# A hybrid decoder block on one core: w_down's difference blocks made in the first stage, and the low parts of k loaded once into half-zero tiles

## The chip, the cores and the metric

The kernel runs on one core of a Trainium2 chip. The core has four engines that the kernel programs separately: TensorE (PE in the profile, with PEld for its weight loads), VectorE (DVE), ScalarE (ACT) and GpSimd (POOL). A fifth, SyncE (SP), issues every DMA of this kernel from one queue, in order. Each engine runs its own instructions strictly in order and waits where one of them needs something that isn't there yet. The metric is the device time of one launch in microseconds; the median of 3 runs before the change is 2561.39 us (2550.47 to 2562.06).

## The reference, cut to what matters

The input x is 2048 tokens by 1024 channels, in float32. One layer:

```python
h = rmsnorm(x, g_mix)
p = h @ w_in                          # 1024 x 2560
a_val, a_gate, b_u, b_v, c_q, c_k, c_v = split(p)
y_a = conformer_conv(a_val, a_gate, ...)      # GLU, causal depthwise conv of 31, layernorm, silu
y_b = chunked_sgu(b_u, b_v, ...)              # gelu, layernorm, 128 x 128 causal mixing
y_c = stick_breaking_attention(c_q, c_k, c_v) # 8 heads of 64; z = q k^T / 8, causal
x = x + concat(rms(y_a), rms(y_b), rms(y_c)) * g_out @ w_out
h = rmsnorm(x, g_ffn)
up = causal_dwconv(h @ w_up)                  # 1024 x 5632, conv width 3
gate, val = split(up)
x = x + (silu(gate) * val) @ w_down           # 2816 x 1024
return rmsnorm(x, g_final)
```

## The kernel before, in words

All products are float32 made of float32r parts. A matrix a is split into a high part (a cast on ACT) and a low part (a minus its high part, on POOL or DVE), and a product is three matmuls: high times high, high times low, low times high (`mm3`, L115 to L117). The work has three stages.

**First stage, 0 to about 530 us.** The input projection, in two halves of 1024 tokens. For each half the columns of w_in come in five groups of 512 (`load_w`): the GLU (columns 0), branch B (512), k (1536), q (1024), v (2048). A group is four tiles `raw` of 512 KB; each is split by ACT (L120, `wh`) and POOL (L121, `wl`). There are two `raw` buffers and five pairs `wh`, `wl`, so only the first tile of a group can be ready while the group before it is in use; the other three follow as PE gives up the old ones. Tokens of x are loaded into the tiles `xi` (pool `xp`, four buffers of 512 KB), normed and transposed (`ptn`). Beside the matmuls DVE runs the convolution of branch A (L344, 31 taps, spread by the generator `conv`), and POOL norms branch B (L292, L295). q, k and v are stored in high and low parts to DRAM: qh_d, ql_d, kh_d, kl_d, v_d.

**Attention, about 515 to 1190 us.** 320 steps: four query blocks of 512 (qs), four head pairs (pr), the key blocks back from the diagonal (kc), two heads (hd), four rows of queries (j). `front` makes z with two matmuls of 128 rows: the stationary tile q of a head holds the high part on 64 rows and the low part on the other 64; it meets `kA` or `kB` (the high part of k, twice, on both halves) in L754 and `lA` or `lB` (the low part, twice) in L757. Then a sigmoid (`om`, ACT L759) and a cumulative product (DVE L762 and L767). Six steps later the result is transposed (`pat`, L780) and split into `ah` and `al`: for two of four on DVE (L793), for two on POOL (L790). Two steps after that it meets v (`po`, L802 and L803). A set of key tiles is loaded by `load_kv`: eight DMAs of 128 KB (four of kh_d, four of kl_d) and one of 512 KB (`vv`), two sets deep. Between the steps the output projection of earlier rows fills PE (`out_proj`, tiles `pab`), with its own loads of y, x and w_out. From step 40 on, every 20th step calls `wd_gen`: `down_blocks` (L605) loads two row blocks of w_down (512 KB each), makes four differences with POOL (L613 to L616) and stores them to wd_d (four DMAs of 256 KB). There are 11 such blocks; the last stage needs them.

**Feed-forward, about 1200 us to the end.** Up and down projections, each with seven block products in place of eight; `down_weights` (L1145) reads wd_d.

What sets the order. The source says in which order work is recorded; a scheduler then lays each engine's instructions out by a timeline of its own, so an engine's queue isn't quite in the order of the source. A tile's next use waits for all readers of its last one.

Of the kernel before, what the change touches and what calls it, by code (L numbers as in the profile page):

```python
# [8 lines left out]
F32 = mybir.dt.float32  # L9
# [6 lines left out]
P = 128  # L16
# [4 lines left out]
def kernel(  # L21
# [68 lines left out]
    def dma32(dst, src):  # L90
        nc.sync.dma_start(dst.bitcast(F32), src.bitcast(F32))
# [259 lines left out]
    def advance(gen, n):  # L351
        for _ in range(n):
            next(gen, None)
# [30 lines left out]
    def branch_b_tail(uv, vh, vl, hf, q4):  # L384
# [14 lines left out]
        branch_rms(yb)  # L399
        return lambda: store_t(yb, 2, hf * HALF + q4 * 512)  # L400

    xs = load_x(0, 0)
    constants()
    V.memset(glu[:, :, 0:HALO], 0.0)
# [42 lines left out]
    def load_kv(tiles, kc, pr):  # L447
        kA, kB, lA, lB, vv = tiles
        k_s = slice(kc * 512, (kc + 1) * 512)
        for hd, th_, tl_ in ((0, kA, lA), (1, kB, lB)):  # L450
            hr = slice(64 * hd, 64 * hd + 64)
            for r in (slice(0, 64), slice(64, 128)):
                dma32(th_[r], kh_d[pr, hr, k_s])
                dma32(tl_[r], kl_d[pr, hr, k_s])
        dma32(
            vv,
            v_d[kc * 4 : kc * 4 + 4, :, pr * 256 : (pr + 1) * 256].rearrange(
                "n p c -> p n c"
            ),
        )  # L460
        return tiles

    for hf in range(2):
# [21 lines left out]
        for q4 in range(2):  # L485
            uv = bp.tile([P, 4, 512], F32, tag="uv", name="uv", bufs=2)
            for j in range(4):
                ps = proj_d(w, hT[q4], j)
                A.activation(uv[:, j, :], ps, AF.Gelu)
                advance(conv, 2)  # L490
                tick()
            uvs.append((uv, *branch_b_norm(uv)))


        for c0, hd, ld in ((1536, kh_d, kl_d), (1024, qh_d, ql_d)):
            w = load_w(c0)
            if hf == 1 and c0 == 1024:

                pre = [
                    bp.tile([P, 4, 512], F32R, tag="uv", name=f"pre{i}", bufs=2)  # L500
                    for i in range(2)
                ]
                first_q = load_q((pre[0][:, 0, :], pre[0][:, 1, :]), 0, 0)
                first_kv = load_kv(
                    (
                        pre[0][:, 2, :], pre[0][:, 3, :], pre[1][:, 0, :],
                        pre[1][:, 1, :],
                        pre[1][:, 2:4, :].rearrange("p a (n c) -> p (a n) c", c=256),
                    ),
                    0, 0,  # L510
                )
            for ct in range(NPAIR):
                for ch in range(2):
                    ps = proj_t(w, ct, hT[ch])
                    eh = ep.tile([P, 512], F32R, tag="eh", name="eh")
                    el = ep.tile([P, 512], F32R, tag="el", name="el")
                    A.copy(eh, ps)
                    V.tensor_tensor(el, ps, eh, op=ALU.subtract)
                    t0 = hf * HALF + ch * 512
                    dma32(hd[ct, :, t0 : t0 + 512], eh)  # L520
                    dma32(ld[ct, :, t0 : t0 + 512], el)
                    advance(conv, 2 if c0 == 1536 else 3)
                    tick()
                    if c0 == 1536 and ct in (0, 2) and ch == 1:
                        after(4, branch_b_tail(*uvs[ct // 2], hf, ct // 2))
# [68 lines left out]
    def load_wo(f):  # L594
# [5 lines left out]
        split_pool(wh, wl, raw)  # L600
        wo_h.append(wh)
        wo_l.append(wl)

    def down_blocks():

        for f in range(NFH):
            r0 = xo.tile([P, D], F32, tag="wd0", name="wd0", bufs=1)
            r1 = xo.tile([P, D], F32, tag="wd1", name="wd1", bufs=1)
            nc.sync.dma_start(r0, w_down_r[f])
            nc.sync.dma_start(r1, w_down_r[NFH + f])  # L610
            b11, b12, b21, b22 = r0[:, 0:512], r0[:, 512:D], r1[:, 0:512], r1[:, 512:D]
            t3 = xo.tile([P, 512], F32, tag="t3", name="wd3", bufs=1)
            G.tensor_tensor(t3, b22, b12, op=ALU.subtract)  # L613
            G.tensor_tensor(b12, b12, b11, op=ALU.subtract)
            G.tensor_tensor(b22, b22, b12, op=ALU.subtract)
            G.tensor_tensor(b21, b21, b22, op=ALU.subtract)  # L616
            for i, t_ in enumerate((b12, b22, t3, b21)):
                nc.sync.dma_start(wd_d[i, :, f, :], t_)
            yield

    def store_blocks(n, he, ho, eng):

# [29 lines left out]
    def out_proj(qs, g, kept=()):  # L652
# [6 lines left out]
        for j in range(4):  # L659
            n = qs * 4 + j  # L660
            x1, (yh, yl) = nxt, ys.pop(0)
            for nh in range(2):
# [57 lines left out]
                        store_blocks(n, even, h, V if qs == NQ - 1 else G)  # L720
                yield

    class Pair:


# [11 lines left out]
    def front(p, kc, hd, j):  # L737
# [2 lines left out]


        if kc not in p.kv:
            kt = [
                kv.tile([P, 512], F32R, tag=n, name=n) for n in ("kA", "kB", "lA", "lB")
            ]
            kt.append(kv.tile([P, 4, 256], F32R, tag="vv", name="vv"))
            p.kv[kc] = load_kv(kt, kc, p.pr)
        kt, lt = p.kv[kc][hd], p.kv[kc][2 + hd]
# [149 lines left out]
    rms_at = {}  # L898
    ready = [out_proj(0, 0), out_proj(1, 0)]
    last_y = []  # L900
    wd_gen = down_blocks()
    for s_ in range(4 * NU + LAG_V):
        if s_ < 4 * NU:
            u, j = divmod(s_, 4)
# [11 lines left out]
                load_vend()  # L916
            if WO_0 <= s_ < WO_0 + 8 * WO_S and (s_ - WO_0) % WO_S == 0:
                load_wo((s_ - WO_0) // WO_S)
        if s_ >= 40 and s_ % 20 == 0:
            next(wd_gen, None)  # L920
        if s_ in rms_at:
            qs = rms_at[s_]
            rcs[qs] = rms_c(sqs[qs])
# [414 lines left out]
```

## Time and profile before

| | us |
|---|---|
| median of 3 runs | 2561.39 |
| profiled execution | 2565.55 |
| its span, first to last instruction | 2563.8 |
| first stage, 0 to 530: PE busy | 493.28 |
| 520 to 640: PE busy | 87.74 of 120 |
| 640 to 960: PE busy | 292.80 of 320 |
| 960 to 1160: PE busy | 190.61 of 200 |
| 1200 to the end: PE busy | 1323.72 of 1364 |

The page reads from the top: the busy time of each engine, then the span in 40 slices of 64 us, in which a digit is a share in tenths. A busy time doesn't say what bounds a stretch; for that the tables by stretch and the lists of waits are read. "PEclk" is the granted TensorE clock as a share of full speed (1.00 is 2.4 GHz, 0.50 is 1.2 GHz). The DMA share is the mean busy share of the 16 DMA engines, so a share near 1 says that no more can be moved in that stretch.

### The profile page before, as it was taken

What the parts mean: (1) busy time and instruction counts of PE and PEld (TensorE: products, weight loads), DVE (VectorE), ACT (ScalarE), POOL (GpSimd) and SP (SyncE); (2) the same over time, 40 slices, a digit from 0 to 9 for tenths busy, and PEclk for the clock granted to TensorE, in tenths of its full rate; (3) what the DMA queues carried; (4) which work ended last, traced back from release to release, by engine and by line L of the source; (5) the groups of instructions that cost most, each with busy time, mean ns of one, the idle gap of its engine ahead of it and who ended that gap; (6) DMA issues with size and microseconds to landing.
All of it is one profiled execution on the core that took longest, in us unless ns stands there. A gap on an engine that the chain in (4) does not pass through costs nothing.

```text
span 2563.8 us, 33236 instructions
## 1 busy us (share of the span) xinstructions
PE 2417.0 (94%) x11139; PEld 1965.9 (77%) x11139; DVE 1857.1 (72%) x2360; ACT 1202.9 (47%) x2138; POOL 1220.7 (48%) x941
## 2 busy tenths in 40 slices
PE   7999999968999889998799999999989999999998
PEld 5878778746777777776588888888867888888887
DVE  3881595356889888995688988874558888888555
ACT  4333522255667657774444444454344344345542
POOL 2433552445457453656154444565424444447551
PEclk9999999979999989998999999999999999999999
DMA  4245426389999998876333333397652333337962
GB/s 138 84 147 168 160 83 181 132 238 261 297 292 288 263 263 220 239 224 207 115 95 106 108 95 106 116 334 230 180 181 78 98 107 104 98 107 224 301 185 100
DMA packets 418235, 445.69 MB, mean 174 GB/s; under 512 B 23922, under 2 KB 301694, under 8 KB 418063
## 3 DMA queue, kind: packets, MB, share of 16 engines
q1 hardware_dynamic: 418063, 443.55, 58.0%
q8 instruction: 89, 1.46, 0.3%
q14 instruction: 83, 0.68, 0.1%
HBM read 305.57 MB, written 137.89 MB: 173 GB/s over the span
## 4 chain that ended last, share of the span: by engine, by line
PE 76%; DMA 8%; DVE 5%; issue 3%; POOL 3%; ACT 2%; SPq 1%; POOLq 0%; DVEq 0%; ACTq 0%
PE prod L115 11%; PE prod L117 11%; PE prod L116 11%; PE pd L117 5%; PE pd L115 5%; PE pd L116 5%; PE pat L780 3%; PE pjt L115 3%; PE pjt L117 3%; PE pjt L116 3%; PE pz L754 2%; PE po L803 1%; PE pab L115 1%; PE pz L757 1%; PE po L802 1%
## 5 line engine op out<-in xcount | busy, mean ns | idle before, releaser
L121 POOL TENSOR_TENSOR wl<-raw,wh 128x512 fp32r<-128x512 f32 (+1 forms) x260 | 383.4, 1477 | 560.6 <-ACT wh L120 548.5
L115 PE MATMUL prod<-thh,wh 128*128 128x512 f32 x1232 | 483.8, 393 | 13.1 <-DVE thl L1049 13.1
L117 PE MATMUL prod<-thh,wl 128*128 128x512 f32 x1232 | 485.1, 394 | 0.0
L116 PE MATMUL prod<-thl,wh 128*128 128x512 f32 x1232 | 482.6, 392 | 0.0
L120 ACT CAST wh<-raw 128x512 fp32r<-128x512 f32 (+1 forms) x260 | 177.4, 684 | 311.8 <-PE prod L116 178.4
L121 POOL TENSOR_TENSOR dwl<-raw,dwh 128x512 fp32r<-128x512 f32 x154 | 223.0, 1479 | 134.5 <-ACT dwh L120 106.2
L115 PEld LDWEIGHTS prod<-thh,wh 128*128 128x128 f32 x1232 | 232.4, 189 | 64.3 <-DVE thl L1049 15.2
L790 POOL TENSOR_TENSOR al<-ar,ah 128x512 fp32r<-128x512 f32 (+2 forms) x160 | 178.7, 1119 | 207.9 <-ACT ah L788 172.3
L116 PEld LDWEIGHTS prod<-thl,wh 128*128 128x128 f32 x1232 | 232.2, 188 | 52.2
L117 PEld LDWEIGHTS prod<-thh,wl 128*128 128x128 f32 x1232 | 232.3, 189 | 50.1
L767 DVE TENSOR_TENSOR_SCAN om<-om,pz 128x512 f32<-128x512 f32 x192 | 240.0, 1269 | 30.3 <-ACT om L759 29.1
L115 PE MATMUL pd<-dwh,sah 128*128 128x512 f32 x616 | 241.2, 392 | 1.3 <-DVE thl L1049 1.2
L117 PE MATMUL pd<-dwh,sal 128*128 128x512 f32 x616 | 242.0, 393 | 0.0
L116 PE MATMUL pd<-dwl,sah 128*128 128x512 f32 x616 | 240.4, 390 | 0.0
L1179 DVE TENSOR_TENSOR sal<-ar,sah 128x512 fp32r<-128x512 f32 x168 | 151.3, 913 | 122.6 <-ACT sah L1178 108.9
L1119 DVE SCALAR_TENSOR_TENSOR cv<-u,vec,cv 128x1024 f32<-128x1024 f32 x176 | 222.5, 1286 | 13.8 <-ACT cv L1117 12.1
L759 ACT ACTIVATE om<-pz 128x512 f32<-128x512 f32 (+2 forms) x320 | 168.6, 544 | 72.6 <-PE pz L757 69.1
L1066 DVE TENSOR_TENSOR u<-prod,u 128x512 f32<-128x512 f32 x220 | 147.2, 686 | 65.5 <-PE prod L117 62.8
L780 PE MATMUL pat<-ident,om 128*128 128x128 f32 x1088 | 179.6, 282 | 5.5 <-DVE al L793 3.7
L780 PEld LDWEIGHTS pat<-ident,om 128*128 128x128 f32 x1088 | 138.7, 145 | 40.9 <-DVE al L793 9.9
L121 POOL TENSOR_TENSOR wl<-s,wh 128x512 fp32r<-128x512 f32 x88 | 122.0, 1387 | 97.5 <-ACT wh L120 97.5
L1178 ACT CAST sah<-ar 128x512 fp32r<-128x512 f32 x168 | 97.1, 583 | 147.8 <-PE pd L116 106.3
(282 smaller groups left out, 5229.6 us busy)
## 6 DMA issues: line engine op xcount, KB each, us to landing
raw<-in_w_up_dram SPq DMA_DIRECT2D x88, 512.0 KB
ar<-s_d SPq DMA_DIRECT2D x112, 256.0 KB
s_d<-act SPq DMA_DIRECT2D x110, 256.0 KB
raw<-in_w_in_dram SPq DMA_DIRECT2D x40, 512.0 KB
raw<-wd_d SPq DMA_DIRECT2D x40, 512.0 KB
vv<-v_d SPq DMA_DIRECT2D x39, 512.0 KB
x_d<-x SPq DMA_DIRECT2D x32, 512.0 KB
raw<-in_w_down_dram SPq DMA_DIRECT2D x30, 512.0 KB
```

The costliest lines, as they stand in the source:

```text
L115: T.matmul(ps, lh, rh, start=start, stop=False)
L116: T.matmul(ps, lh, rl, start=False, stop=False)
L117: T.matmul(ps, ll, rh, start=False, stop=stop)
L120: A.copy(hi, src)
L121: G.tensor_tensor(lo, src, hi, op=ALU.subtract)
L759: A.activation(om, pz[:, :w_], AF.Sigmoid, scale=-0.125)
L767: V.tensor_tensor_scan(om[:, ::-1], om[:, ::-1], pz[:, ::-1], initial=p.carry[hd, j], op0=ALU.mult, op1=ALU.bypass,)
L780: T.transpose(pt[:, j * P : (j + 1) * P], a4[j][:, b * P : (b + 1) * P], ident)
L790: G.tensor_tensor(al[:, c_], ar[:, c_], ah[:, c_], op=ALU.subtract)
L1066: V.tensor_tensor(dst, ps, other, op=ALU.add)
L1119: V.scalar_tensor_tensor(cv, u[:, j : j + HALF], cw(j), cv, op0=ALU.mult, op1=ALU.add)
L1179: V.tensor_tensor(lo, ar, hi, op=ALU.subtract)
```

## The change

`down_blocks` moves to the first stage. It takes its two tiles from the pool of `xi`, needs no third tile (the differences are made in place, in another sequence), and yields twice a block: after the loads, and after the stores. It is called 12 times in each half: once after every second row of branch B's projection and once after every second product of k and of q. That makes 24 calls for the 22 halves of 11 blocks. The calls in the attention go.

`load_kv` stores the low part of k once, on the 64 rows where the stationary tile holds the high part of q; the other 64 rows of `lA` and `lB` are zeroed once and stay zero. For that `lA` and `lB` become two fixed pairs, used in turn, where they were tiles of a pool with two buffers. With it the product of the two low parts, which was part of z before, is left out.

```diff
+    def down_blocks():
+        for f in range(NFH):
+            r0 = xp.tile([P, D], F32, tag="xi", name="wd0")
+            r1 = xp.tile([P, D], F32, tag="xi", name="wd1")
+            nc.sync.dma_start(r0, w_down_r[f])
+            nc.sync.dma_start(r1, w_down_r[NFH + f])
+            yield
+            b11, b12, b21, b22 = r0[:, 0:512], r0[:, 512:D], r1[:, 0:512], r1[:, 512:D]
+            for i, t_, u_, v_ in (
+                (0, b12, b12, b11), (1, b22, b22, b12), (3, b21, b21, b22),
+                (2, b11, b22, b11),
+            ):
+                G.tensor_tensor(t_, u_, v_, op=ALU.subtract)
+                nc.sync.dma_start(wd_d[i, :, f, :], t_)
+            yield
+    wd_gen = down_blocks()
...
             for r in (slice(0, 64), slice(64, 128)):
                 dma32(th_[r], kh_d[pr, hr, k_s])
-                dma32(tl_[r], kl_d[pr, hr, k_s])
+            dma32(tl_[hr], kl_d[pr, hr, k_s])
...
                 A.activation(uv[:, j, :], ps, AF.Gelu)
                 advance(conv, 2)
+                advance(wd_gen, j % 2)
...
+                G.memset(pre[1][64:128, 0, :].bitcast(F32), 0.0)
+                G.memset(pre[1][0:64, 1, :].bitcast(F32), 0.0)
                 first_q = load_q((pre[0][:, 0, :], pre[0][:, 1, :]), 0, 0)
...
                     advance(conv, 2 if c0 == 1536 else 3)
+                    advance(wd_gen, ch)
...
+    lows, turn_l = [], [0]
+    for i in range(2):
+        lows.append([kv.tile([P, 512], F32R, tag=f"{n}{i}", name=f"{n}{i}", bufs=1) for n in ("lA", "lB")])
+        for hd, t_ in enumerate(lows[i]):
+            zr = slice(64 * (1 - hd), 64 * (1 - hd) + 64)
+            G.memset(t_[zr].bitcast(F32), 0.0)
...
-            kt = [
-                kv.tile([P, 512], F32R, tag=n, name=n) for n in ("kA", "kB", "lA", "lB")
-            ]
+            kt = [kv.tile([P, 512], F32R, tag=n, name=n) for n in ("kA", "kB")]
+            kt += lows[turn_l[0] % 2]
+            turn_l[0] += 1
...
-        if s_ >= 40 and s_ % 20 == 0:
-            next(wd_gen, None)
```

How the queues stand. SP's queue in the first stage, before, from the constants of the feed-forward on: `xi` are the tokens of the second half, `raw` the rest of the weights up to k's first products, whose stores come next.

```order
19 L180 DMA r__596<-in_ffn_conv_b_dram 44x128
20 L211 DMA xi<-in_x_dram 128x1024 x4
21 L246 DMA raw<-in_w_in_dram 128x2x512 x8
22 L91 DMA kh_d<-eh 128x512 x2
23 L91 DMA kl_d<-el 128x512 x2
```

The same place now; a wd tile with a number is one block's half.

```order
19 L180 DMA r__596<-in_ffn_conv_b_dram 44x128
20 L407 DMA wd_685<-in_w_down_dram 128x1024
21 L408 DMA wd_686<-in_w_down_dram 128x1024
22 L407 DMA wd_837<-in_w_down_dram 128x1024
23 L408 DMA wd_838<-in_w_down_dram 128x1024
24 L417 DMA wd_d<-wd_685 128x512
25 L417 DMA wd_d<-wd_686 128x512 x2
26 L417 DMA wd_d<-wd_685 128x512
27 L407 DMA wd_1022<-in_w_down_dram 128x1024
28 L417 DMA wd_d<-wd_837 128x512
29 L408 DMA wd_1023<-in_w_down_dram 128x1024
30 L246 DMA raw<-in_w_in_dram 128x2x512
```

The first six blocks now stand where the four tiles of tokens stood, with the weights between them; the tokens follow behind the sixth block.

POOL's queue at the change from the GLU's weights to branch B's, before: the `wl` are the low parts of weight tiles, `rs` and `uv` belong to branch B's norm.

```order
12 L194 AFFINE_SELECT wsm<-wsr 128x128 x4
13 L121 TENSOR_TENSOR wl<-raw,wh 128x1024 x4
14 L112 TENSOR_TENSOR rs_755<-tm_754,mhalf 128x4
15 L292 TENSOR_TENSOR uv<-uv,ln_119 128x4x256
16 L295 TENSOR_TENSOR uv<-uv,ln_120 128x4x256
```

The same place now.

```order
12 L194 AFFINE_SELECT wsm<-wsr 128x128 x4
13 L416 TENSOR_TENSOR wd_685<-wd_685 128x512
14 L416 TENSOR_TENSOR wd_686<-wd_686,wd_685 128x512
15 L416 TENSOR_TENSOR wd_686<-wd_686 128x512
16 L416 TENSOR_TENSOR wd_685<-wd_686,wd_685 128x512
17 L416 TENSOR_TENSOR wd_837<-wd_837 128x512
18 L121 TENSOR_TENSOR wl<-raw,wh 128x1024
19 L416 TENSOR_TENSOR wd_838<-wd_838,wd_837 128x512
20 L121 TENSOR_TENSOR wl<-raw,wh 128x1024
21 L416 TENSOR_TENSOR wd_1022<-wd_1022 128x512
22 L416 TENSOR_TENSOR wd_838<-wd_838 128x512
23 L416 TENSOR_TENSOR wd_837<-wd_838,wd_837 128x512
```

The splits of the weights, which stood together, now have differences between them, and all six blocks of this half are made by the second row of `uv`.

SP's queue in the attention, before, some way into the second query block.

```order
285 L91 DMA kA<-kh_d 64x512
286 L91 DMA lA<-kl_d 64x512
287 L91 DMA kA<-kh_d 64x512
288 L618 DMA wd_d<-wd_5069 128x512
289 L91 DMA lA<-kl_d 64x512
290 L91 DMA yh_d<-ych 128x512
291 L618 DMA wd_d<-wd_5065 128x512
```

And a like place now.

```order
371 L91 DMA kA<-kh_d 64x512 x2
372 L91 DMA lA_4199<-kl_d 64x512
373 L91 DMA yh_d<-ych 128x512
374 L91 DMA qA<-qh_d 64x512
```

One load of the low part stands where two stood, and the stores of wd_d are gone.

## Rows read from the trace of the kernel before

**Rows 1.** The page: the DMA share in tenths, 40 slices of 64 us.

```profile
DMA  4245426389999998876333333397652333337962
```

**Rows 2.** Stretches: busy us (count) of PE, PEld, DVE, ACT, POOL; clock; DMA share; GB/s.

```profile
520.00:640.00 120.00, 87.74 (x397) 68.40 (x396) 74.34 (x96) 63.01 (x142) 58.21 (x49) 0.84 0.97 253
640.00:960.00 320.00, 292.80 (x1524) 237.85 (x1523) 271.33 (x305) 206.50 (x432) 175.38 (x154) 0.95 0.97 280
960.00:1160.00 200.00, 190.61 (x1039) 154.15 (x1038) 181.42 (x197) 148.75 (x298) 109.33 (x92) 1.00 0.81 227
```

**Rows 3.** w_down's differences: ns, min/median/max, first and last start.

```profile
L613 POOL TENSOR_TENSOR wd<-wd,wd x11: 1262/1288/1300, 619.2 to 948.6; 128x512 f32<-128x512 f32 x11
```

**Rows 4.** Waits of PE, 520 to 640: us in total, times, longest.

```profile
PE pz L754 <- DMA kA<-kh_d: 12.6, 4, 4.8
```

**Rows 5.** Waits of PE, 640 to 960.

```profile
PE po L803 <- POOL al L790: 12.6, 5, 4.9
...
PE po L802 <- DMA vv<-v_d: 2.4, 1, 2.4
```

**Rows 6.** DMA, 520 to 640: bytes, then issues with count and size.

```profile
DMA packets 21229, 30.41 MB, mean 253 GB/s; under 512 B 2063, under 2 KB 11791, under 8 KB 21222
...
lA<-kl_d SPq DMA_DIRECT2D x14, 128.0 KB
...
lB<-kl_d SPq DMA_DIRECT2D x12, 128.0 KB
...
wd<-in_w_down_dram SPq DMA_DIRECT2D x2, 512.0 KB
wd_d<-wd SPq DMA_DIRECT2D x3, 256.0 KB
```

**Rows 7.** DMA, 640 to 960.

```profile
DMA packets 59211, 89.62 MB, mean 280 GB/s; under 512 B 5808, under 2 KB 31322, under 8 KB 59184
...
wd_d<-wd SPq DMA_DIRECT2D x41, 256.0 KB
...
wd<-in_w_down_dram SPq DMA_DIRECT2D x20, 512.0 KB
...
lB<-kl_d SPq DMA_DIRECT2D x40, 128.0 KB
...
lA<-kl_d SPq DMA_DIRECT2D x40, 128.0 KB
```

**Rows 8.** Two stretches of the first stage, columns as in Rows 2.

```profile
80.00:120.00 40.00, 40.00 (x178) 33.14 (x177) 36.47 (x45) 12.41 (x15) 16.61 (x8) 1.00 0.13 40
...
200.00:240.00 40.00, 40.00 (x180) 33.02 (x179) 3.73 (x8) 9.47 (x14) 12.17 (x7) 1.00 0.46 138
```

**Rows 9.** SP: the load of the second half's tokens before.

```profile
64.48 1.77 SPq L211 DMA_DIRECT2D xi<-in_x_dram  x4
```

**Rows 10.** The chain that ended last, 100 to 136 us: start, duration.

```profile
105.53 2.40 POOL uv L292
...
118.86 4.13 DMA raw<-in_w_in_dram
...
126.50 1.04 POOL rs L112
```

**Rows 11.** The same chain later: a store of 256 KB.

```profile
477.22 2.01 DMA vr_d<-vs
```

**Rows 12.** PE at the first change of weights: the first matmul with branch B's weights.

```profile
75.65 0.39 PE L115 MATMUL pjd<-wh,hTh 128*128 128x512 f32 x1
```

**Rows 13.** POOL at that change: start, duration.

```profile
73.61 4.76 POOL L121 TENSOR_TENSOR wl<-raw,wh 128x1024 fp32r<-128x1024 f32 x2 [26.90 <-ACT wh L120]
81.08 2.40 POOL L121 TENSOR_TENSOR wl<-raw,wh 128x1024 fp32r<-128x1024 f32 x1 [2.70 <-ACT wh L120]
```

**Rows 14.** POOL at the same change in the second half.

```profile
320.23 4.77 POOL L121 TENSOR_TENSOR wl<-raw,wh 128x1024 fp32r<-128x1024 f32 x2 [20.21 <-ACT wh L120]
```

**Rows 15.** Branch A's convolution on DVE: ns, min/median/max.

```profile
L344 DVE SCALAR_TENSOR_TENSOR pc<-glu,vec,pc x116: 1257/1290/1292, 72.6 to 413.3; 128x1024 f32<-128x1024 f32 x116
```

More of the change, by code (lines that the diff above doesn't have):

```diff
@@ L602, in load_wo @@
         wo_l.append(wl)
[L604 to L619, printed above, removed]
     def store_blocks(n, he, ho, eng):
@@ L900 @@
     last_y = []
-    wd_gen = down_blocks()
     for s_ in range(4 * NU + LAG_V):
```

## Prediction

> **What bounds the kernel now.** I read the page's slices first, then a table by stretch, the waits of PE in two of the stretches, and what the DMA engines moved in them. The slices show one plateau of full DMA engines, from the end of the first stage through two thirds of the attention [rows 1]. The stretches give it sizes [rows 2]: from 520 to 640 us the DMA share is 0.97, PE is busy for 87.74 of 120 us and its granted clock averages 0.84 of 2.4 GHz; from 640 to 960 the share is again 0.97, PE is busy for 292.80 of 320 at 0.95. From 960 to 1160, when the last of w_down's differences has started (at about 950 us [rows 3]), the share is 0.81 and PE busy for 190.61 of 200 at 1.00. So the attention has a part that is short of transfers and a part where PE is the bound, and the change takes bytes from the first. In 520 to 640 PE's waits say so: 12.6 us on kA [rows 4]. In 640 to 960 they say it only in part: 2.4 us on vv, but 12.6 on `al` from POOL [rows 5], in whose queue w_down's differences stand.
>
> **The base.** The sum is made against the profiled execution, 2565.55 us with a span of 2563.8. It stands 4.2 us above the median of the runs, 2561.39; I take that off at the end.
>
> **520 to 640 us.** What goes: half of the 26 loads of low parts, 13 x 0.131 = 1.70 MB; two loads of w_down, 1.05 MB; three stores to wd_d, 0.79 MB; together 3.54 of 30.41 MB [rows 6], at 253 GB/s 14.0 us. PE could take all of it, since it idles 120 - 87.74 = 32 us and loses 87.74 x 0.16 = 14 to the clock. I take two thirds, -9, since less than half of the idle time names a transfer [rows 4]. Bounds: 0 (PE waits for kA's loads, and those stay) and -18 (fewer waits bring the clock back as well).
>
> **640 to 960 us.** What goes: half of 80 low parts, 5.2 MB; 20 loads of w_down, 10.5 MB; 41 stores, 10.7 MB; together 26.5 of 89.62 MB [rows 7], at 280 GB/s 94 us. The other 63.1 MB need 225 us at that rate, so transfers no longer bound the stretch, and PE is late next. It issued 1524 matmuls here and 1039 in the 200 us that follow [rows 2]; at that rate 1524 take 293 us, 27 fewer. The other way: 292.80 x 0.95 = 278 us of full clock, at the later busy share of 190.61 / 200 = 0.953, give 292. The new stretch would move 63.1 MB in 292 us, 216 GB/s, under the 227 of the one it is compared with, and DVE would be busy for 271.33 / 292 = 0.93 against 181.42 / 200 = 0.91: the comparison is fair, with DVE a little short. POOL gives up 41 differences of 1.288 us [rows 3], 53 us, that stood before `al`; this works in the same 27 and is not added. I take three quarters, -20, as the two stretches don't run the same mix of fill and attention. Bounds: -5 (vv's wait and a fifth of `al`'s) and -30 (the clock as well).
>
> **After 960 us.** Only low parts go, where PE is already at 0.953 and its clock at 1.00 [rows 2]: -1, between 0 and -4. The feed-forward keeps its order and reads the same wd_d: 0.
>
> **The first stage pays.** 11 blocks come in, with two loads, four differences and four stores each, through SP's one queue and POOL's. The DMA engines have room, a share of 0.13 and 0.46 in two stretches [rows 8]. The question is who stands behind the blocks in the two queues.
>
> First half. The tokens' tiles come free at 64.5 us, when the next tokens were loaded [rows 9]; now two blocks are. With 4.13 us for a load of 512 KB [rows 10], 1.29 for a difference [rows 3], 2.01 for a store of 256 KB [rows 11] and about 1 for issues, a pair of tiles takes 4.1 + 5.2 + 2.0 + 1 = 12.3 us a turn, and two pairs work at once: 6.2 us a block, six in 37 us. From about 69 that is 106; four splits of weights share POOL meanwhile, 2.4 us each, so 106 to 115.
>
> Behind them stand the splits of branch B's weights. PE turned to those at 75.65 [rows 12]. It runs three products side by side (three PSUM tiles), 18 matmuls a tile, at 40.00 / 180 = 0.222 us each [rows 8]; the fourth tile's low part is needed after 54 of them, at 87.6, and was there at 81.08 + 2.40 = 83.5 [rows 13]. Now ten differences and two splits stand before it: 69 + 10 x 1.29 + 3 x 2.4 = 89. PE loses 1 to 2 us.
>
> Behind the sixth block stands branch B's norm, `uv`, which began at 105.53, and behind that the splits of k's weights; the second `rs` followed at 126.50 [rows 10], and DVE's queue (k's low parts among it) and then PE waited for it. If `uv` slips by 4 to 8 us, this slips by about 3, as POOL had gaps between. The tokens of the second half now load behind block six, at about 115 us, and are wanted only with the third row of v's product, three groups of weights later: that hides them.
>
> Second half. Five blocks take 31 us. POOL makes three of them ahead of the splits of branch B's weights, which began at 320.23 [rows 14], and two between those: 1 to 2 us again.
>
> The zeroing is six memsets on 64 rows x 512, not seen before; the nearest row is a difference on 128 rows, so 0 to 8 us of POOL. I take 0: they run where POOL is busy for 58.21 of 120 us [rows 2]; without that cover it would be 8.
>
> I take +5 for the first stage. Bounds: 0 (all of it in POOL's and DVE's gaps) and +22 (both halves lose a turn of 12.3 us less the margin, and the lost time comes back as a lower clock).
>
> A rule speaks against this part. Branch A's convolution on DVE had 116 instructions between 1257 and 1292 ns [rows 15], beside a POOL that was busy for 17 of 40 us or idle alike. The Trainium skill, GPSIMD Engine Reference, Key points, says that GpSimd shares its SBUF interfaces with VectorE and contends with VectorE instructions that have two SBUF inputs. The convolution reads its sum from PSUM, so it has one, and the trace agrees: its spread is 3%. By the rule alone, if it took hold of every difference, 44 x 1.29 = 57 us would be lost to DVE in a stage where it is busy for 36.47 of 40 us; by the row, nothing. That is a rival below.
>
> **The sum.** -9 - 20 - 1 + 5 = -25; 2565.55 - 25 = 2540.5; less 4.2, 2536.
>
> **Rivals.**
>
> *Deeper gain, 2514.* Every term at its far end but the first stage: -18 - 30 - 4 + 5 = -47. For it: the clock of 0.84 and 0.95 on the plateau, and SP's shorter queue. Against: the stretch after 960 still has PE idle at 5%, with DVE at 0.91.
>
> *The transfers were hidden anyway, 2559.* If PE's idle time on the plateau comes from the sequence of DVE, ACT and POOL, the bytes are worth the named waits at most: about a third of the 12.6 on kA and the 2.4 on vv, -7; with the first stage's +5 that is -2. For it: from 640 to 960 the largest wait names POOL, and transfers that were issued early enough can fill the DMA engines without holding anyone. Against: the same sequence reaches 0.953 as soon as the share falls to 0.81.
>
> *SP's head of line, slower, 2581.* A store to wd_d waits at the head of SP's queue for POOL, and the next weights' loads wait behind it. If a block takes 12 us, not 6.2 (one pair of tiles in flight, since each new load stands behind the other pair's stores), six end at 69 + 72 = 141, where `uv` and the splits of k's weights were due from 105: PE would stand for some 25 us in the first half and as long in the second, and of the attention's gain of 30 nothing is left: +20. It decides from about 9 us a block: then six end at 123, and the splits of k's weights, the second of which was ready at 118.86 [rows 10], are late by more than a margin of 4. For it: the loads of the third block stand behind stores of the first two in SP's new order. Against: SP and POOL have long gaps in the first stage.
>
> *DVE shares with POOL, 2551.* If each difference stretches DVE's work by its own 1.29 us, 24 in the first half cost it 31 us and 20 in the second 26. DVE has gaps later (3.73 of 40 us busy from 200 to 240 [rows 8]), so PE sees about a quarter, +15. Against it stands the spread of the convolution [rows 15]. This is what the Trainium skill's rule in the GPSIMD Engine Reference, Key points, would make of the change.
>
> *The change doesn't do what it says*, a low part still loaded twice: the two queues in front of this show one load where two stood, so I give it nothing.
>
> **How the numbers follow.** The forecast has 0.53, with 2522 to 2552 as its own range (the terms at half their bounds, not all to one side); deeper gain 0.17; hidden transfers 0.17; SP's queue 0.08; DVE 0.05. About 0.5%, 13 us, is what a measurement of this kernel can tell from no change, so faster means under 2548.6: 0.48 of the forecast, all of the deeper gain, 0.05 of the hidden transfers (whose loss in the first stage may be 0) and 0.02 of DVE's case, 0.72. Slower, over 2574, is SP's queue, 0.08. The rest is the same, 0.20. The range of 2508 to 2562 holds the forecast and most of the deeper gain, of the hidden transfers and of DVE's case; it leaves out SP's queue and the ends of the others.
>
> **What would show it.** Right: from 520 to the end of the attention a shorter stretch, with the DMA share at 0.8 to 0.9 and PE's clock near 1; PE's waits on kA and on `al` shrink; the attention begins about 5 us later than before. Wrong: SP waiting on POOL's differences for tens of us in 65 to 130 or 300 to 380, with PE idle at a change of weights; or a DMA share well under 0.97 on the plateau while PE idles as before.

## The result and the profile after

The changed kernel takes 2528.72 us (median; 2524.30 to 2532.71) beside 2560.88 for the kernel before in the same rounds: a ratio of 0.9888, 95% interval 0.9859 to 0.9917. That is 32 us less by the medians, or 1.1% by the ratio. A second set of runs gave 2533.93 beside 2557.50, ratio 0.9901 (0.9880 to 0.9922). The profiled execution is 2528.20 us, its span 2526.5.

The plateau of full DMA engines is gone from the attention after 640 us, and part of what was moved stands now near 100 and 300 us. First the page's DMA share, to be held against [rows 1]:

```profile
DMA  4845655479767668757133333596552323337962
```

Then the stretches, columns as in [rows 2]; two of the first stage and the three of the attention.

```profile
80.00:120.00 40.00, 40.00 (x177) 32.92 (x176) 33.84 (x41) 7.58 (x10) 33.69 (x24) 1.00 0.88 295
120.00:160.00 40.00, 32.05 (x135) 25.21 (x134) 33.67 (x42) 12.00 (x20) 22.57 (x11) 0.96 0.42 134
...
520.00:640.00 120.00, 94.35 (x432) 75.24 (x431) 86.31 (x106) 65.14 (x150) 56.08 (x51) 0.80 0.94 268
640.00:960.00 320.00, 308.00 (x1705) 252.82 (x1704) 298.48 (x333) 233.59 (x486) 139.58 (x125) 1.00 0.70 205
960.00:1160.00 200.00, 185.63 (x983) 148.27 (x982) 166.10 (x186) 137.92 (x276) 121.89 (x103) 0.98 0.69 207
```

From 640 to 960 the DMA share falls from 0.97 to 0.70, the granted clock goes from 0.95 to 1.00 of 2.4 GHz, and PE issues 1705 matmuls where it issued 1524 [rows 2]. From 520 to 640 little changes: the share is 0.94, the clock 0.80. From 80 to 120 the DMA share is 0.88, where it was 0.13, and POOL's busy time has doubled [rows 8]. In the next 40 us PE issues 135 matmuls; before it issued 155:

```profile
120.00:160.00 40.00, 36.64 (x155) 29.81 (x154) 37.07 (x44) 8.12 (x16) 15.05 (x8) 0.91 0.37 118
```

To see where the time went, I followed single matmuls by their place in the program: the last z of the first pair, the first z of the second query block, the 17th z of the fourth block, the last z against `kA`. First of before, then of after (start, duration):

```profile
521.26 0.78 PE L754 MATMUL pz<-pre 128*128 128x512 f32 x1
...
590.63 0.30 PE L754 MATMUL pz<-kA,qA 128*128 128x128 f32 x1 [1.21 <-DMA kA<-kh_d]
...
962.23 0.40 PE L754 MATMUL pz<-kA,qA 128*128 128x512 f32 x1
...
1159.21 0.39 PE L754 MATMUL pz<-kA,qA 128*128 128x512 f32 x1
```

```profile
526.13 0.78 PE L769 MATMUL pz<-pre 128*128 128x512 f32 x1
...
588.91 0.44 PE L769 MATMUL pz<-kA,qA 128*128 128x128 f32 x2
...
926.09 0.40 PE L769 MATMUL pz<-kA,qA 128*128 128x512 f32 x1
...
1121.45 0.40 PE L769 MATMUL pz<-kA,qA 128*128 128x512 f32 x1
```

The attention starts 4.9 us later and its last z comes 37.8 earlier. With the starts of the third and fourth query block between them, for all runs (us; z are counted by their matmuls with the high part of k, and the 17th of the fourth block is the one that stood nearest to 960 us before):

| kernel | first pair's last z | 2nd block | 3rd | 4th | its 17th z | last z |
|---|---|---|---|---|---|---|
| before | 521.3 | 590.6 | 736.6 | 929.3 | 962.2 | 1159.2 |
| changed | 526.1 | 588.9 | 724.4 | 898.6 | 926.1 | 1121.5 |
| changed, again | 529.2 | 589.2 | 727.0 | 904.3 | 931.8 | 1127.7 |
| blocks moved, lows as before | 526.4 | 603.5 | 729.4 | 901.7 | 929.2 | 1124.3 |
| lows once, blocks as before | 520.8 | 585.5 | 726.0 | 913.4 | 948.1 | 1146.3 |
| no differences | 522.0 | 591.7 | 733.1 | 923.0 | 951.2 | 1146.8 |
| transfers moved | 515.6 | 589.0 | 722.5 | 901.6 | 929.1 | 1124.5 |
| blocks behind the splits | 544.2 | 608.7 | 744.1 | 921.5 | 949.0 | 1145.5 |
| w_out later | 532.3 | 594.6 | 722.7 | 898.4 | 926.0 | 1121.1 |
| both edits | 541.5 | 595.6 | 740.2 | 912.2 | 939.7 | 1136.1 |
| four and seven | 526.3 | 582.6 | 720.8 | 894.9 | 922.4 | 1118.7 |
| four, four and three | 520.3 | 585.6 | 719.8 | 894.5 | 922.0 | 1118.6 |
| the same, again | 519.7 | 581.4 | 716.9 | 891.6 | 919.1 | 1115.7 |

Two profiles of the changed kernel differ by up to 6 us here, so a difference of that size in one profile proves nothing alone. The second block's start is the least firm: between it and the z before it lie 2 to 13 us (13 in the run with blocks moved), by how much other work of PE stands there. The profile of the blocks behind the splits is of an execution of 2548.73 us, 7 above that kernel's median. From the last z to the end nothing changed: the page's span less the last z is 1404.6 before and 1405.0 after.

PE's waits in the attention after; from 520 to 640, then from 640 to 960 (us in total, times, longest):

```profile
PE pz L772 <- DMA lA<-kl_d: 6.4, 3, 2.4
```

```profile
PE pz L769 <- DVE om L782: 4.7, 12, 1.0
```

The 12.6 us on kA [rows 4], the 12.6 on POOL's `al` and the 2.4 on vv [rows 5] are gone. From 640 to 960 no wait on a transfer is left; the largest is on DVE's cumulative product. From 520 to 640 a transfer still leads the list. SP's queue shows the same turn: from 640 to 960 it now waits 92.6 us for PE to give up key tiles, where it waited 15.2 before.

```profile
SPq L91 <- PE pz L772: 92.6, 49, 6.0
```

### The profile page after: what moved, and what is told of

It is laid out like the page before. It is cut to its first block, busy times and chain, and to the rows that moved or that the text cites. A ratio compares the mean times of both kernels' runs of the same rounds, so it can differ in the third digit from the quotient of the medians.

```text
span 2526.5 us, 33097 instructions
## 1 busy us (share of the span) xinstructions
PE 2399.1 (95%) x11139; PEld 1955.8 (77%) x11139; DVE 1862.6 (74%) x2360; ACT 1201.8 (48%) x2138; POOL 1222.1 (48%) x947
## 4 chain that ended last, share of the span: by engine, by line
PE 75%; DVE 8%; DMA 7%; POOL 3%; ACT 3%; issue 3%; SPq 1%; DVEq 0%; POOLq 0%; ACTq 0%
PE prod L115 11%; PE prod L117 11%; PE prod L116 11%; PE pd L117 5%; PE pd L115 5%; PE pd L116 5%; PE pat L795 3%; PE pjt L115 3%; PE pjt L117 3%; PE pjt L116 3%; DVE om L782 2%; PE pz L769 2%; PE pz L772 2%; DVE om L777 2%; PE po L818 1%
## 5 line engine op out<-in xcount | busy, mean ns | idle before, releaser
L115 PE MATMUL pd<-dwh,sah 128*128 128x512 f32 x616 | 241.3, 392 | 1.3 <-DVE thl L1061 1.2
```

Of the source, the lines that this page charges most:

```text
L115: T.matmul(ps, lh, rh, start=start, stop=False)
```

## The experiments

My theory: the bytes taken out of the full stretch are the gain. The rivals: POOL's own 53 us of differences held `al`, and they are the gain; or the low parts alone did it. That `al` was late because a difference at the head of POOL's queue waited for its block came to me with the results; the expectations below still put `al`'s wait down to POOL's work. For the cost: the differences stand ahead of branch B's norm in POOL's queue; or else SP's queue, the DMA engines, or DVE.

**Blocks moved, low parts as before.** The changed kernel with this edit (and `lA`, `lB` from the pool again, without the zeroing):

```diff
-            dma32(tl_[hr], kl_d[pr, hr, k_s])
+                dma32(tl_[r], kl_d[pr, hr, k_s])
```

> The change with w_down's blocks in the first stage alone; the low parts of k are loaded twice as before. Theory of the transfers (the attention is short of DMA until 960 us, and every byte that leaves it counts until PE is the bound): 21 of the 26.5 MB that leave 640 to 960 are the blocks', so most of the gain comes: 2535 to 2542 us, DMA share on 640 to 960 at 0.75 to 0.85. Theory of POOL (the gain is the 53 us of differences that stood before al): the whole gain of this part of the attention, 2530 to 2536, with the DMA share of no account. Theory of hidden transfers: 2555 to 2560.

Measured: 2529.08 us (2525.68 to 2533.04) beside 2561.4, ratio 0.9875 (0.9857 to 0.9894). The blocks alone give the whole gain. It is more than the theory of the transfers had allowed (2535 to 2542) and nearer to that of POOL (2530 to 2536), so this run doesn't tell the two apart; the next ones do.

**Low parts once, blocks as before.** The kernel before with the changed `load_kv`, the zeroed tiles, and nothing else.

> The change with the low parts of k loaded once alone; w_down's blocks stay in the attention. Theory of the transfers: 5.2 MB less from 640 to 960 at 280 GB/s is up to 19 us, 1.7 MB less from 520 to 640 up to 7, so 2538 to 2550, DMA share still over 0.9 to 960 us. Theory of POOL: nothing of POOL's work goes, so 2555 to 2561. If the two halves of the change add up, this run and that with the blocks alone give together what the whole gives, 32 us; if both only serve to bring the transfers under PE's bound, their sum is larger than the whole.

Measured: 2549.32 (2541.80 to 2553.23), ratio 0.9952 (0.9934 to 0.9970): 12 us. By parts the sum would be 32 + 12 = 44; both together give 32, and 24 in the second set of runs. They pay for the same shortage. The stretch from 640 to 960 says so; here blocks moved, then low parts once (columns as in [rows 2]):

```profile
640.00:960.00 320.00, 309.63 (x1710) 254.50 (x1709) 293.62 (x334) 230.67 (x478) 136.64 (x123) 1.00 0.83 229
```

```profile
640.00:960.00 320.00, 295.54 (x1568) 240.43 (x1569) 279.46 (x307) 210.47 (x440) 186.22 (x156) 0.96 0.86 257
```

With the blocks gone a share of 0.83 no longer holds PE: busy for 309.63 of 320, against 308.00 in the changed kernel with its 0.70. What the low parts then take off the queue is room that nobody waits for. With the blocks in place the share of 0.86 isn't enough, for another reason: PE's wait on POOL's `al` is still there, 12.9 us.

```profile
PE po L813 <- POOL al L800: 12.9, 5, 6.3
```

**No differences.** The kernel before without POOL's 44 differences; loads and stores of the blocks stay.

```diff
-            G.tensor_tensor(t3, b22, b12, op=ALU.subtract)
-            G.tensor_tensor(b12, b12, b11, op=ALU.subtract)
-            G.tensor_tensor(b22, b22, b12, op=ALU.subtract)
-            G.tensor_tensor(b21, b21, b22, op=ALU.subtract)
```

> The kernel before with w_down's four differences left out: the blocks are loaded and stored from the attention as before, 22 MB, without POOL's 44 instructions (57 us), so wd_d holds plain blocks of w_down. Theory of the transfers: the bytes are all there, DMA share 0.97 until 960, gain 0 to 6: 2555 to 2561. Theory of POOL: most of the gain of the blocks' part, 2538 to 2546.

Measured: 2551.46 (2545.12 to 2552.82), ratio 0.9957 (0.9939 to 0.9974): 10 us, not 30, more than the transfers' theory had here (0 to 6) and less than POOL's (15 to 23). The wait on `al` is gone, and with it SP's 16.7 us behind POOL's differences, so while the transfers stay, the two together are worth no more than 10. In its place PE waits for v, at a DMA share of 1.02 (a share that reads a little over 1 is a full one):

```profile
PE po L797 <- DMA vv<-v_d: 8.5, 5, 3.8
```

**Transfers moved, differences kept in the attention.** The blocks' loads and stores run in the first stage, at the changed kernel's places and without differences; the 44 differences stay at the 20th steps of the attention, on two tiles that are loaded once.

> The counterpart: the blocks' loads and stores move to the first stage without the differences (wd_d holds plain blocks), and POOL's 44 differences stay in the attention, on two tiles that are loaded once. Low parts of k as before. Theory of the transfers: as the blocks moved whole or better, since the first stage doesn't wait for POOL, 2533 to 2542; al's waits on POOL stay. Theory of POOL: 2553 to 2561. The first stage shows by its end (the last z of the first head pair) what of its 5 us was POOL's.

Measured: 2531.57 (2528.02 to 2533.95), ratio 0.9883 (0.9865 to 0.9901): 30 us, with POOL as busy in the attention as before, and just under the transfers' 2533 to 2542. That `al`'s waits would stay was wrong. Columns as in [rows 2], then PE's wait on `al`, then in the first stage POOL's first norm of branch B:

```profile
640.00:960.00 320.00, 306.90 (x1666) 251.57 (x1665) 287.94 (x323) 225.45 (x467) 177.74 (x153) 0.98 0.78 222
```

```profile
PE po L821 <- POOL al L808: 1.1, 2, 0.8
```

```profile
104.51 2.41 POOL L292 TENSOR_TENSOR uv<-uv,ln 128x1024 f32<-128x1024 f32 x1 [1.59 <-DVE uv L288]
```

POOL is busy for 177.74 us, 175.38 before [rows 2], and `al` is in time. So the differences' work alone didn't hold `al`. In the kernel before, the longest of the five waits shows what did: POOL stood idle until a block's load had landed, made one difference, and only then `al` (PE's `po`, then POOL):

```profile
849.30 0.69 PE L803 MATMUL po<-al,vv 128*128 128x384 f32 x1 [4.95 <-POOL al L790]
```

```profile
847.03 1.26 POOL L613 TENSOR_TENSOR wd<-wd,wd 128x512 f32<-128x512 f32 x1 [7.38 <-DMA wd<-in_w_down_dram]
848.25 0.99 POOL L790 TENSOR_TENSOR al<-ar,ah 128x384 fp32r<-128x384 f32 x1
```

Ahead of three of the other four POOL was idle before a difference too, for 4.2 to 5.5 us, though there the profile names other releasers. And `uv` starts at 104.51, and the first pair's last z comes at 515.6, although the same bytes go through SP and the DMA engines from 65 us on: by themselves the transfers don't cost the first stage anything.

**Blocks behind the splits.** To win back the first stage's 5 us I took the blocks up from k's products on only, and queued each difference on POOL behind the last split of weights:

```diff
-                advance(wd_gen, j % 2)
...
-                    advance(wd_gen, ch)
+                    advance(wd_gen, 1)
...
-                G.tensor_tensor(t_, u_, v_, op=ALU.subtract)
+                with tc.issue_after(last_split[0].ins):
+                    G.tensor_tensor(t_, u_, v_, op=ALU.subtract)
```

> The changed kernel, all of its work kept, with each of w_down's differences queued on POOL behind the last split of weights that was written before it, and the blocks taken up only from k's products on: branch B's first norm (`uv`) and the splits of k's weights stand ahead of all differences again. Theory (the first stage's +5 is POOL's queue: differences that wait for their loads ahead of the norm and the splits): `uv` begins near 105 again, not 116.8; the first pair's last product z near 519 to 522, not 526.1; and the time falls by as much, to 2522 to 2525. Rival A (the transfers that follow, 520 to 620 us at a DMA share near 1, take the earlier start back): `uv` and z earlier as said, but the time stays at 2527 to 2530. Rival B (SP's queue or the DMA engines cost the 5 us): z stays at 524 to 527, and the time too.

Measured: 2541.40 (2540.43 to 2548.73), ratio 0.9924 (0.9905 to 0.9943): 9 us slower than the changed kernel by the ratios, 13 by the medians, which none of the three had expected. `uv` is early, as the theory said, and the first pair's last z comes 18 us later all the same (15 in the profile of both edits, below). The norm, the stretch from 200 to 240, and what DVE waited for from 120 to 260:

```profile
105.37 2.41 POOL L294 TENSOR_TENSOR uv<-uv,ln 128x1024 f32<-128x1024 f32 x1 [2.78 <-issue]
```

```profile
200.00:240.00 40.00, 39.22 (x178) 32.23 (x177) 7.94 (x14) 10.67 (x18) 20.83 (x17) 1.00 1.03 342
```

```profile
DVE el L543 <- DMA yl_d<-yl: 14.8, 3, 7.6
...
DVE el L543 <- DMA ql_d<-el: 7.7, 2, 7.4
```

Eight blocks now pass in the first half, between 126 and 223 us, where k, q and branch B are stored. The low parts' tiles of k and q (`el`) come free when their stores have landed, and those now share SP's queue and the engines with the blocks: a share of 1.03 from 200 to 240 (0.46 before [rows 8]). (It moves 342 GB/s there, where a share of 0.97 moved 253 in [rows 2]: a full share isn't a fixed rate.) In the changed kernel DVE's `el` waits 2.7 us on yl_d in the same time and nothing on ql_d. The place costs more than the queue order gives. But that isn't all of the 18 us: this profile is 8.7 us behind the changed kernel's at the first of branch B's mixing products of the second half (`pm`, 390.7 against 382.0) and loses 9.4 more from there to the last z. The edit changed the order of POOL's queue, the place and the number of blocks in each half at once, and no run separates these.

**w_out later.** The changed kernel, with 2.5 MB fewer to load at the attention's start:

```diff
-            if s_ == 0:
+            if s_ == 64:
                 nc.sync.dma_start(gffn_b, g_ffn[0].partition_broadcast(P))
...
-            if WO_0 <= s_ < WO_0 + 8 * WO_S and (s_ - WO_0) % WO_S == 0:
-                load_wo((s_ - WO_0) // WO_S)
+            if s_ in (2, 5, 8, 11, 40, 46, 52, 58):
+                load_wo((2, 5, 8, 11, 40, 46, 52, 58).index(s_))
```

> The changed kernel, all of its work kept, with 2.5 MB of loads taken out of the start of the attention: the second half of w_out (four loads of 512 KB, which only the second halves of the output product use) at steps 40, 46, 52 and 58 instead of 14 to 23, and the gain of the feed-forward norm (512 KB) at step 64 instead of 0. Theory (520 to 620 us is still bound by bytes: a DMA share near 1 at 261 to 264 GB/s, PE's clock at 0.72 there): 2.5 MB at 262 GB/s are 9.5 us; about half to two thirds show, so z of the second query block begins 5 to 7 us earlier, and the time is 2520 to 2524. Rival (the sequence of the first query blocks, short chains of z, mask, transposes, sets the pace there, and lA's wait would only change its name): within 2 us of the changed kernel, 2526 to 2531.

Measured: 2526.76 (2520.91 to 2528.79), ratio 0.9859 (0.9839 to 0.9880). That is in the rival's range, and the second block's z came at 594.6, not 5 to 7 us earlier; but the edit didn't do what it was for. The bytes moved from 530 to 620, in the changed kernel and here:

```profile
DMA packets 17538, 23.91 MB, mean 266 GB/s; under 512 B 1533, under 2 KB 10756, under 8 KB 17531
```

```profile
DMA packets 18119, 24.59 MB, mean 273 GB/s; under 512 B 1614, under 2 KB 10858, under 8 KB 18112
```

The first stage ends 6 us later in this profile (532.3), so the two stretches don't hold quite the same work; but the room was filled again, by loads of later steps as far as the bytes tell, so the edit didn't make the stretch less full, and it can't say what a less full one would be worth.

**Both edits.** The last two together.

> Both edits, w_down's differences queued behind the splits and the 2.5 MB of loads later; all of the work kept. If both terms are real and stand apart: 2514 to 2519. If the full DMA engines after 520 us swallow the earlier start: alone the first edit gives nothing, and here 3 us or more beyond the loads' edit, since there is room then. If neither is real: 2526 to 2531.

Measured: 2540.50 (2535.12 to 2541.96), ratio 0.9913 (0.9895 to 0.9931), within none of the three expectations. It follows the first of the two; the second adds nothing that can be measured.

**Four blocks and seven.** The blocks at the changed kernel's places, but four in the first half and seven in the second:

```diff
+    left = [8, 14]
+
+    def advance_wd(hf, n):
+        n = min(n, left[hf])
+        left[hf] -= n
+        advance(wd_gen, n)
...
-                advance(wd_gen, j % 2)
+                advance_wd(hf, 1 if hf else j % 2)
...
-                    advance(wd_gen, ch)
+                    advance_wd(hf, ch)
```

> The changed kernel, all of its work kept, with four of w_down's blocks in the first half of the first stage and seven in the second, not six and five. Theory (each block that POOL makes ahead of branch B's first norm costs about 7 us of queue, and the norm has a slack that four blocks use up): in the first half `uv` begins near 105 again (116.8 in the changed kernel) and the second half's tokens are normed near 247, not 251.6; in the second half two more blocks, 14 us, end near 355, so that `uv` there starts at 357 to 362 and the 5 us are lost there: time 2526 to 2531, no gain. Rival (the loss doesn't come from the norm's place in POOL's queue but from the DMA engines or DVE): the first half's tokens at 250 to 252 as in the changed kernel, whatever `uv` does.

Measured: 2525.00 (2523.55 to 2525.62), ratio 0.9867 (0.9844 to 0.9891). In the first half `uv` starts at 103.97, and `rs` of branch A's norm at 244.93 (251.64 in the changed kernel, 246.73 before; the expectation calls it the tokens' norm). PE begins to transpose the second half's tokens there at 239.5 (246.8 in the changed kernel, 241.3 before). In the second half `uv` starts at 359.56, PE's wait for `el` is 6.8 us, not 2.8, and the first pair's last z is at 526.3 again. Both halves did what the queue theory says; the time is 1 us under its range.

**Four, four and three.** As that, with `left = [8, 8]`, `advance_wd(hf, j % 2)`, and the last three blocks made in the attention as the kernel before makes them, at steps 80, 100 and 120.

> As the run with four and seven, but four blocks in the first half, four in the second and the last three in the attention, one at steps 80, 100 and 120, behind the stretch in which the DMA engines are full; all of the work kept. Theory (POOL's queue in front of the norm costs the 5 to 6 us of the first stage, and from 640 on the DMA share of 0.70 has room for three blocks): the first pair's last z at 520 to 523, not 526.1, and the gain stays: 2522 to 2525. Rival A (full DMA engines from 530 to 620 take the earlier start back, as after the run that kept the differences in the attention): z earlier, the time 2527 to 2531. Rival B (three blocks in the attention cost what all eleven did there in proportion, 3/11 of 32): 2532 to 2536.

Measured: 2521.18 (2519.38 to 2524.83), ratio 0.9854 (0.9832 to 0.9875), just under the theory's 2522 to 2525. `uv` starts at 104.92, and the first pair's last z at 520.32. From 640 to 960:

```profile
640.00:960.00 320.00, 309.54 (x1700) 254.91 (x1699) 292.69 (x331) 231.44 (x479) 145.17 (x130) 0.99 0.75 221
```

The attention starts where it started before the change, and three blocks in it cost PE nothing that can be measured (309.54 against 308.00 us busy, and from the first pair's last z to the last z 598.3 us against 595.3 and, in the second profile of the changed kernel, 598.5). They come where the DMA share has room: it is 0.75 with them.

**The two side by side.** Its lead over the changed kernel is small, and the two had not run beside each other, so both ran again in turn on one chip.

> The changed kernel once more, beside the next run on the same chip and in the same rounds. Expected 2526 to 2531 us (2528.7 before).

> The kernel with four, four and three blocks once more, in the same rounds as the changed kernel. If its gain is real (the norm's place in POOL's queue, kept by the room after 640 us): 4 to 8 us under the changed kernel, 2519 to 2525, with the first pair's last z near 520 again. If its 2521 was chance or the chip's: within 2 us of the changed kernel.

Measured: 2533.93 (2531.53 to 2535.62) and 2521.24 (2517.25 to 2524.17), ratios to before of 0.9901 (0.9880 to 0.9922) and 0.9852 (0.9825 to 0.9879). No run of the one reaches one of the other. The changed kernel is 3 us over what I had expected of it, so the lead of 12.7 us is more than the 4 to 8 expected; it was 7.5 between the earlier medians. The first pair's last z is 9.5 us earlier and the last z 12.0.

## Why the prediction was right, point by point

The mechanism was right and the total 7 us short: 2536 forecast, 2528.72 measured, inside the forecast's own range. The term that was furthest off is that of 640 to 960. By its terms, with the sizes from the table of z above (changed kernel less before; the two profiles lie 37 us apart and the medians 32, so these sizes add up to 37):

- **First stage, +5: 4.9 measured, 7.9 in the second profile; the path is the forecast one, its parts mis-sized.** Where the loss arises: in the first half PE waits 8.0 us between 60 and 160 us, where it waited 3.2 before; it begins to transpose the second half's tokens 5.5 us later (246.8, 241.3 before), and in the second half its waits from 260 to 400 grow only from 5.9 to 7.2. PE's waits from 60 to 160, after, then before:

```profile
PE pm L115 <- DVE el L541: 4.1, 1, 4.1
PE pjt L117 <- POOL wl L121: 1.7, 2, 1.2
PE pjt L115 <- ACT wh L120: 1.5, 1, 1.5
PE pm L115 <- ACT uv L509: 0.7, 1, 0.7
```

```profile
PE pm L115 <- DVE el L518: 3.2, 1, 3.2
```

  The longest, on `el`, was there before and grew by 0.9. New are the waits for the parts of k's weights (`wh`, `wl`), 3.2 us, and 0.7 for `uv`. The chain from the blocks to these weights, in the changed kernel (start, duration, what):

```profile
73.47 2.49 DMA wd_d<-wd
...
76.93 5.25 DMA wd<-in_w_down_dram
...
84.47 3.27 DMA wd_d<-wd
...
88.95 4.74 DMA wd<-in_w_down_dram
...
96.85 2.54 POOL wd L416 x2
...
100.49 5.92 DMA wd_d<-wd
...
107.38 5.39 DMA wd<-in_w_down_dram
...
114.28 2.54 POOL wd L416 x2
116.82 2.37 POOL uv L292
...
119.26 2.41 POOL uv L295
...
121.69 1.06 ACT vh L120
...
125.19 2.34 POOL wl L121
```

  POOL's queue behind the blocks is what the prediction named. The six blocks take 47.4 us, 7.9 each (from 69.4 to 116.8), not 6.2, and end just behind the 106 to 115 that it gave; `uv` slips by 11.3 us, not 4 to 8, the splits of k's weights by 8.7 (125.16, 116.42 before), and the second `rs` by 8.2 where 3 were expected, from [rows 10]. The blocks were slow by their own transfers: the chain's three stores and three loads take 27.1 us, where the store of 2.01 [rows 11] and the load of 4.13 [rows 10] would give 18.4. Those rows come from stretches with a DMA share of 0.42 (460 to 500) and 0.26 (100 to 140); from 80 to 120 it is now 0.88. So transfers that hold nobody by themselves (the run with transfers moved) do hold whatever stands behind a difference in POOL's queue. With four blocks in front (the runs with four) `uv` is on time. Of the parts, the 1 to 2 us at branch B's weights didn't come (PE waits for nothing there up to 120 us) and the norm's share is larger than 3; that they gave 5 together is partly luck. The six memsets took 0.52 us each, 3 in all, and no wait names them.

- **520 to 640, -9: -6.6, and -9.3 in the second profile.** From the first pair's last z to the second block's first, 69.4 us became 62.8. "PE could take all of it" failed: the room didn't stay empty. The stretch moved 32.19 MB, more than the 30.41 of before [rows 6], because loads of later steps came forward; the share stayed at 0.94 and the clock at 0.80.

- **640 to 960, -20: about -30, and -25 in the second profile.** From the second block's first z to the 17th of the fourth, 371.6 us became 337.2, -34.4, and 320 of the 371.6 are this stretch. The bytes were foreseen well: 65.73 MB were moved (63.1 forecast), by a stretch that also got further. The discount to three quarters wasn't needed: the DMA share fell to 0.70, not to 0.8 to 0.9, the clock reached 1.00 and PE is busy for 0.963 of the stretch, above the 0.953 that I had compared with. The prediction put `al`'s wait down to POOL's 53 us of work; the runs without differences and with transfers moved show that POOL's waiting for the blocks held it. That it adds nothing of its own to the gain was right.

- **After 960, -1: -1.6, and -1.1 in the second profile** (from the 17th z of the fourth block to the last z, 197.0 us became 195.4). From the fourth block's first z the gain is 7 us, but 5.4 of it lie before the 17th, from 929 to 962 us, where the kernel before still made its last differences (the last begins at 955.7). With the blocks moved alone this piece takes 27.5 us as in the changed kernel, with the low parts alone 34.7, before 32.9.

- **Feed-forward, 0:** 0.4 us.

The rivals. *The transfers were hidden anyway* falls with the run that moved the transfers alone and was 30 us faster. *SP's head of line* had the right place and too high a price: SP waited for POOL's differences 32 times in the first stage, 30.3 us in all, but never over 1.6 us, and the 7.9 us a block stay under the 9 from which it was to decide. The sign that the prediction had named for this case, SP waiting for tens of us with PE idle at a change of weights, is there in small: 15.2 us from 65 to 130 and as much from 300 to 380, with PE's 3.2 at k's weights.

```profile
SPq L417 <- POOL wd L416: 30.3, 32, 1.6
```

*DVE shares with POOL* falls by the convolution, which ran beside 44 differences and took what it took before [rows 15]:

```profile
L344 DVE SCALAR_TENSOR_TENSOR pc<-glu,vec,pc x116: 1251/1290/1292, 73.3 to 419.2; 128x1024 f32<-128x1024 f32 x116
```

The rule of the Trainium skill (GPSIMD Engine Reference, Key points) is that POOL contends with VectorE instructions that have two SBUF inputs; the convolution has one, and the row agrees with the rule so far. No run here tries it on instructions with two. *Deeper gain* was right on its largest term, -30 (25 to 30 measured), and wrong on the plateau's beginning.

What stays open is why PE is busy for only 94 of the 120 us after 520: the run that was to thin out its transfers didn't thin them out.

## What to carry to other kernels

A transfer's price hangs on how full the DMA engines are in the place it is put in: eleven blocks of 2.1 MB cost the attention 30 us at a share of 0.97, and three of them nothing measurable at 0.75. In the first stage the transfers of six blocks a half cost nothing by themselves; with their differences in POOL's queue six cost 5 us and four nothing, since the norm and the next weights' splits stand behind them. Take a transfer's duration for an estimate from a stretch that is as full as the new place will be, and check what stands behind it in order on every engine that handles it. Before a wait is called an edit's cost, look whether it was there before. When two edits relieve the same shortage, price them together: 32 and 12 us alone were 32 and, measured again, 24 together.

## What had not been expected of the hardware

A wait of 4.1 us on PE costs more than itself. After the one on `el` above, the matmuls of 512 columns follow each other at 0.43 us, and some 3.7 us after its end at 0.23; the changed kernel's chain further on, then two stretches (columns as in [rows 2]):

```profile
141.06 0.45 PE pm L115
...
142.57 0.43 PE pjt L115
...
145.20 0.24 PE pjt L116
```

```profile
141.00:144.60 3.60, 3.54 (x12) 3.06 (x13) 3.53 (x5) 0.47 (x1) 3.02 (x2) 0.53 0.91 336
145.00:150.00 5.00, 5.00 (x23) 4.10 (x22) 3.45 (x7) 1.05 (x4) 2.41 (x1) 1.00 0.00 0
```

The granted clock is 0.53 in the first and 1.00 in the second, so nearly all of the first passes at the lower of the clock's two levels, 1.2 GHz. Five matmuls of 512 columns at 0.43 are 0.2 us late each, and six of 256 columns at 0.21 about 0.1 each (they follow each other at 0.12 before the wait): some 1.6 us on top of the 4.1. A shorter wait needn't cost less: in the kernel before, after the 3.2 us on `el`, the granted clock is 0.50 from 134 to 140 us, and about ten matmuls of 512 columns pass at that pace. Where a term of a sum is an idle time of PE, this comes on top of it.
